# Log-sum-exp over rows on one core: a small Ln moved from ahead of the last exp to behind it

## The chip, the cores and the metric

One core of one Trainium2 chip. The metric is the device time of one execution in microseconds (us), median of several runs; lower is better. Two times are kept apart below: the time of a run (162.5 us) and the span of the profiled execution (161.2 us, the instructions alone).

## The reference

```python
x = np.random.randn(32, 512, 1024).astype(np.float32)       # axis = -1
x_max = np.max(x, axis=axis, keepdims=True)
return (x_max.squeeze(axis) + np.log(np.sum(np.exp(x - x_max), axis=axis))).astype(np.float32)
```

16384 rows of 1024 numbers: 128 rows on each of 128 partitions. The kernel leaves out the maximum and computes log(sum(exp(x))).

## The kernel before

The input comes in 17 chunks of rows through a ring buffer. ScalarE takes the exp. The sums of most rows are made by VectorE, those of the others by ScalarE itself: an exp with an accumulator output, followed by a read of the accumulator. The last four chunks have one row each and go the second way, with their sums in the tile `late`, which lies in PSUM; the ring, the other sums (`sums`) and the result (`res`) lie in SBUF. Both are memories on the chip. Three Ln instructions make the result: 81 rows in the middle of the kernel, 43 rows near its end, the last 4 rows at the end.

```python
CHUNKS = [                       # rows, rows summed by VectorE, parts, by halves
    (4, 4, 1, False), (15, 15, 1, False), ...
    (7, 7, 1, True), (5, 4, 1, True), (4, 3, 1, True), (3, 3, 1, False), (2, 2, 1, True),
    (1, 0, 1, False), (1, 0, 1, False), (1, 0, 1, False), (1, 0, 1, False),
]
LATE = 4
...
    def take_logs(lo, hi, src, dve_wait, act_wait):
        nonlocal acts
        nc.scalar.wait_ge(act_done, act_wait)
        nc.scalar.wait_ge(dve_done, dve_wait)
        nc.scalar.activation(out=res[:, lo:hi], in_=src, func=Ln).then_inc(act_done, 1)
        acts += 1
...
    for i, (r, n_dve, parts, by_halves) in enumerate(CHUNKS):
        if i:
            load(i)
        s, row = place[i]
        ...
        if i == len(CHUNKS) - 1:
            take_logs(logged, late_row, sums[:, logged:late_row], *done_before[-LATE])
        nc.scalar.wait_ge(landed[i], 16)
        ...                                  # exps whose sums VectorE makes
        for j in range(n_dve, r):
            nc.scalar.activation(out=ring[:, s + j], in_=ring[:, s + j], func=Exp,
                                 accum_out=total(row + j)).then_inc(act_done, 1)
            acts += 1
        done_before.append((dves, acts))

    take_logs(late_row, NB, late[:, : NB - late_row], dves, acts)
    nc.sync.wait_ge(act_done, acts)
    nc.sync.dma_start(out=out_v, in_=res).then_inc(stored, 16)
```

The softmax here doesn't subtract the row's maximum and nothing guards it: scores larger than these inputs give would overflow.

## Time and profile before

| | before |
|---|---|
| time, first three runs | 162.53 us median (162.44 to 162.91) |
| span of the profiled execution | 161.2 us |
| DMA of the input | 67.11 MB, mean 417 GB/s over the span |
| ScalarE (ACT) / VectorE (DVE) busy | 115.1 / 121.0 us |

The page's totals and slices, the chain and ScalarE's timeline of the tail stand in the prediction.

### The profile page before, as it was taken

How to read it: one execution, taken by the hardware profiler on the slowest of the kernel's cores; microseconds unless marked ns; L12 is line 12 of the kernel's file. 1: busy time of each engine (PE TensorE's matmuls, PEld its weight loads, DVE VectorE, ACT ScalarE, POOL GpSimd, SP SyncE). 2: the span in 40 equal slices, each digit the busy share in tenths (PEclk: the TensorE clock that was granted, in tenths of full speed). 3: DMA queues.
4: the chain of work that ended last, by engine and by line, in shares of the span. 5: the costliest groups of instructions: out<-in, count | busy, mean ns of one | idle time of the engine just before them, and what ended most of it. 6: DMA issues, size and time to landing. Idle time of an engine off the chain costs nothing.

```text
span 161.2 us, 149 instructions
## 1 busy us (share of the span) xinstructions
DVE 121.0 (75%) x46; ACT 115.1 (71%) x40; POOL 0.2 (0%) x4
## 2 busy tenths in 40 slices
DVE  0028000003999999999999699999999999999892
ACT  3170005996079960999419993999199999999995
POOL 0000000000000000000000000000000000000000
DMA  7999699899899899899889999999899999999990
GB/s 260 504 488 488 290 442 520 374 407 520 374 407 520 374 407 520 374 407 520 374 374 455 455 455 439 423 423 423 385 439 430 434 441 413 418 431 415 409 406 32
DMA packets 2592, 67.18 MB, mean 417 GB/s; under 512 B 288, under 2 KB 416, under 8 KB 928
## 3 DMA queue, kind: packets, MB, share of 16 engines
q1 hardware_dynamic: 2592, 67.18, 97.2%
HBM read 67.11 MB, written 0.07 MB: 417 GB/s over the span
## 4 chain that ended last, share of the span: by engine, by line
DMA 48%; DVE 29%; ACT 20%; issue 0%
DMA ring<-in_x_dram 48%; DVE sums L157 29%; ACT ring L137 17%; ACT ring L164 3%; ACT res L108 0%
## 5 line engine op out<-in xcount | busy, mean ns | idle before, releaser
L157 DVE TENSOR_REDUCE sums<-ring 128x8 f32<-128x8192 f32 (+5 forms) x14 | 111.2, 7994 | 37.1 <-ACT ring L137 37.0
L137 ACT ACTIVATE ring<-ring 128x8192 f32<-128x8192 f32 (+6 forms) x18 | 104.4, 5835 | 43.1 <-DMA ring<-in_x_dram 42.9
L144 DVE CUSTOM_DVE_ANT_0 ring<-ring 128x512 f32<-128x512 f32 x16 | 9.9, 686 | 0.0
L164 ACT ACTIVATE ring<-ring 128x1024 f32<-128x1024 f32 x9 | 9.3, 1042 | 0.0
L122 ACT ACT_TABLE_LOAD x1 | 1.3, 1283 | 1.4 <-PEq L70 1.4
L164 ACT ACTIVATION_READ_ACCUMULATOR ring<-ring 128x1 f32 x9 | 1.6, 174 | 0.0
L144 DVE DVE_READ_ACCUMULATOR2_ANT sums<- 128x1 f32 x16 | 1.3, 83 | 0.0
L108 ACT ACTIVATE res<-sums 128x81 f32<-128x81 f32 (+1 forms) x2 | 0.5, 248 | 0.0
L108 ACT ACTIVATE res<-late 128x4 f32<-128x4 f32 x1 | 0.2, 173 | 0.0
L209 POOL MEMSET const-bfloat16-1.0<- 128x1 bf16 x1 | 0.1, 101 | 0.0
L209 POOL MEMSET const-uint8-127<- 128x1 uint8 x1 | 0.1, 101 | 0.0
L209 POOL MEMSET const-float32-0.0<- 128x1 f32 x1 | 0.1, 98 | 0.2 <-issue 0.2
L209 POOL MEMSET const-float32-1.0<- 128x1 f32 x1 | 0.1, 98 | 0.0
## 6 DMA issues: line engine op xcount, KB each, us to landing
ring<-in_x_dram SPq DMA_DIRECT2D x1, 7680.0 KB, 24.4
ring<-in_x_dram SPq DMA_DIRECT2D x1, 7168.0 KB, 28.6
ring<-in_x_dram SPq DMA_DIRECT2D x1, 6656.0 KB, 35.7
ring<-in_x_dram SPq DMA_DIRECT2D x1, 4608.0 KB, 20.3
ring<-in_x_dram SPq DMA_DIRECT2D x2, 2048.0 KB, 16.0
ring<-in_x_dram SPq DMA_DIRECT2D x1, 3584.0 KB, 28.3
ring<-in_x_dram SPq DMA_DIRECT2D x1, 2560.0 KB, 27.3
ring<-in_x_dram SPq DMA_DIRECT2D x4, 512.0 KB, 27.0
```

The costliest lines, as they stand in the source:

```text
L108: nc.scalar.activation(out=res[:, lo:hi], in_=src, func=Ln).then_inc(act_done, 1)
L122: nc.scalar.preload_act_table_set("natural_log_exp_and_others")
L137: nc.scalar.activation(out=ring[:, s + lo : s + hi], in_=ring[:, s + lo : s + hi], func=Exp).then_inc(act_done, 1)
L144: nc.vector.tensor_tensor_reduce(out=ring[:, s + j, : D // 2], in0=ring[:, s + j, : D // 2], in1=ring[:, s + j, D // 2 :], scale=1.0, scal ...
L157: nc.vector.reduce_sum(out=sums[:, row + lo : row + hi], in_=ring[:, s + lo : s + hi], axis=AX).then_inc(dve_done, 1)
L164: nc.scalar.activation(out=ring[:, s + j], in_=ring[:, s + j], func=Exp, accum_out=total(row + j),).then_inc(act_done, 1)
L209: nc = _bacc.Bacc("TRN2", target_bir_lowering=False, num_devices=1)
```

## The change

Its intent: behind the last exp ScalarE waits for the read of its accumulator before it can take the last Ln. The Ln of 43 rows, whose sums are ready earlier, is to fill that wait, in place of delaying the last exp.

```diff
-        if i == len(CHUNKS) - 1:
-            take_logs(logged, late_row, sums[:, logged:late_row], *done_before[-LATE])
         nc.scalar.wait_ge(landed[i], 16)
...
-    take_logs(late_row, NB, late[:, : NB - late_row], dves, acts)
+    last_sum = acts
+
+    take_logs(logged, late_row, sums[:, logged:late_row], *done_before[-1 - LATE])
+    take_logs(late_row, NB, late[:, : NB - late_row], dves, last_sum)
```

The last Ln still waits for the last accumulator's read (`last_sum`), not for the moved Ln.

## The prediction

> **What bounds the kernel now.** I read the page from the top, then the chain of waits, then ScalarE's own timeline of the last microseconds, and last the raw record of the same trace, which has nanoseconds and the semaphore instructions that the views leave out.
>
> The page's totals and slices:
>
> ```profile
> span 161.2 us, 149 instructions
> ...
> DVE 121.0 (75%) x46; ACT 115.1 (71%) x40; POOL 0.2 (0%) x4
> ...
> DVE  0028000003999999999999699999999999999892
> ACT  3170005996079960999419993999199999999995
> POOL 0000000000000000000000000000000000000000
> DMA  7999699899899899899889999999899999999990
> GB/s 260 504 488 488 290 442 520 374 407 520 374 407 520 374 407 520 374 407 520 374 374 455 455 455 439 423 423 423 385 439 430 434 441 413 418 431 415 409 406 32
> ```
>
> A slice is 161.2 / 40 = 4.03 us. The DMA row is full until the last slice: the kernel streams 67 MB in at about 420 GB/s, and the input load alone fills some 157 of the 161 us. Only in the last slice does DMA fall to 0 and ScalarE (ACT) still works. So the body is a stream from memory, and the change, which touches two small Ln instructions of ScalarE, can only act in the tail after the stream. One of the Lns (128x43) and its place are all that moves; loads, exps and VectorE's sums stay in order, as the comparison of the two programs' instruction lists shows.
>
> The chain of work that ended last, its final pieces (columns: start us, duration us, what):
>
> ```profile
> 146.98 2.76 ACT ring L137
> 149.74 1.04 ACT ring L164 x2
> 150.78 4.46 ACT ring L137 x2
> 155.24 3.02 ACT ring L164 x6
> 158.25 0.01 ACT res L108
> 158.26 0.01 issue
> 158.28 1.11 ACT ring L164 x2
> 159.39 0.02 issue
> 159.42 0.17 ACT res L108
> ```
>
> From 146.98 us the chain is ScalarE without a break: the data for the last chunks had landed and ScalarE works through a backlog. Whatever shortens ScalarE's sequence here shortens the kernel. The piece "ACT res L108" is given 0.01 us only, because the chain hands time to the instructions by their overlapping ends; what the Ln really pushes has to be read from start to start, in ScalarE's timeline of the tail (start, duration):
>
> ```profile
> 156.14 1.04 ACT L164 ACTIVATE ring<-ring 128x1024 f32<-128x1024 f32 x1
> 157.09 0.16 ACT L164 ACTIVATION_READ_ACCUMULATOR ring<-ring 128x1 f32 x1
> 157.14 1.05 ACT L164 ACTIVATE ring<-ring 128x1024 f32<-128x1024 f32 x1
> 158.09 0.17 ACT L164 ACTIVATION_READ_ACCUMULATOR ring<-ring 128x1 f32 x1
> 158.14 0.24 ACT L108 ACTIVATE res<-sums 128x43 f32<-128x43 f32 x1
> 158.28 1.04 ACT L164 ACTIVATE ring<-ring 128x1024 f32<-128x1024 f32 x1
> 159.22 0.16 ACT L164 ACTIVATION_READ_ACCUMULATOR ring<-ring 128x1 f32 x1
> 159.42 0.17 ACT L108 ACTIVATE res<-late 128x4 f32<-128x4 f32 x1
> ```
>
> An exp with its accumulator's read takes 1.00 us from start to start (156.14, 157.14, 158.14). The last exp starts 1.14 us after the one before it, because Ln 128x43 sits between: 0.14 us. After the last exp comes the only gap: the read starts at 159.22, and the last Ln, which needs that read's result, not before 159.42.
>
> **What the Trainium skill says, and whether this trace agrees.** "Perfetto Trace Analysis", section "DVE / Act Engine Instruction (TENSOR_ADD, Activation, etc)": a record runs from the start in the ALUs to the acknowledgement of the write, at which the semaphore is pushed; the next instruction may prefetch before that. The trace agrees: an exp starts some 0.05 us after the start of a read whose record lasts 0.16 us, but the last Ln, which waits for the read's semaphore, starts only after the read's end. In the raw record that end is 159.226 + 0.158 = 159.384 us and the Ln starts at 159.417, 33 ns later.
>
> "ScalarE: Activation LUTs", section "What ACT_TABLE_LOAD costs": an activation takes 186 ns + 0.833 ns per element, and back-to-back ones overlap by about 93 ns. For 1024 elements that is 1039 ns (the page: 1042). For 43 it is 222 ns (the trace: 241); the overlap here is 241 - 142 = 99 ns. The same page's section on table sets has exp and Ln in one set, and the trace has one table load, at the start, with Exp and Ln already interleaved; another order adds none.
>
> "Advanced Engine Details and Errata", section "Engine Queue Depths": ScalarE queues 8 instructions, so waits can be met ahead of time. The trace agrees so far: the separate wait of the last Ln for VectorE passed at 158.249 us, 1.17 us before that Ln started.
>
> "DMA: Bandwidth & Descriptors", section "Anatomy of one DMA": about 2 us fixed for a transfer, mostly the receipt of the write. It tells of another issuing path; here the store is issued at 159.616 and the wait for it ends at 161.178, 1.56 us, and nothing in the change touches it.
>
> **The change, part by part**, from the raw record's nanoseconds.
>
> 1. Removed: Ln 128x43 ahead of the last exp. It started at 158.138 and the exp at 158.280, so it held the exp back by 142 ns. Without it the exp starts one exp period after the exp before: 157.140 + 0.998 (the period from 157.140 to the Ln's start at 158.138) = 158.138 us. Gain of this step: 0.142 us.
>
> 2. Read of the last accumulator: it started 946 ns after its exp (158.280 to 159.226) and took 158 ns. Now 158.138 + 0.946 = 159.084, ending at 159.242.
>
> 3. Added: the same Ln 128x43 behind that read. It does not wait for it: its waits are for sums finished before. As in the kernel before, it starts 51 ns after the read's start (158.087 to 158.138): 159.084 + 0.051 = 159.135. Its 142 ns from start to start free the engine at 159.277.
>
> 4. The last Ln needs both: the read's semaphore, 159.242 + 0.033 = 159.275, and a free engine, 159.277. They meet within 2 ns, so the Ln of 43 rows fills the wait almost exactly: start at about 159.28, against 159.417. Net 0.14 us earlier. (Without the moved Ln the gap from read start to last Ln is 191 ns; an instruction that needs 51 + 142 = 193 ns fits in it.)
>
> 5. Everything behind moves along: last Ln 173 ns, store issue, 1.56 us to the store's landing. The span becomes 161.19 - 0.14 = 161.05 us, and the time 162.53 - 0.14 = 162.39 us.
>
> Beside the path: VectorE's last sum, which Ln 128x43 needs, ends at 157.960 + 0.081 = 158.041. ScalarE's wait for it passed at 158.073 and the Ln started at 158.138, so it held nothing up by more than the few ns by which I cannot tell a decode from a wait. In the changed kernel this sum has one more exp, 1 us, to spare.
>
> **The rivals.**
>
> *The wait is only exchanged: the moved Ln delays the last one.* If the last Ln, queued behind it, cannot have its wait checked until the moved one has ended, it starts at 159.135 + 0.241 + 0.033 = 159.409, and the gain is 8 ns. For it: the queue is in order. Against it: ScalarE's exp started at 158.280 while the Ln before it ended at 158.379, so an end of record doesn't block the next one. The time would be 162.5.
>
> *A wait on VectorE was part of the path.* The wait's pass at 158.073 is only 65 ns ahead of the Ln's start. In an execution in which VectorE ends a little later, the kernel before is held there and the changed one is not; the gain would be 0.14 us plus that lag, perhaps 0.2 in all (an estimate: 0.14 plus an equal 65 ns), time 162.3. Against it: the start at 158.138 follows the read by the same 51 ns as the exps follow theirs.
>
> *The store hides it.* If the store's landing depended on the end of the last loads, ScalarE's end would not matter. Against it: the DMA row is at 0 in the last slice, and the store is issued 26 ns after the last Ln's end at 159.590. I give it little.
>
> *The noise is greater than the effect.* The three runs of before lie between 162.44 and 162.91, 0.47 us apart, over three times the gain. A median of a few runs can then fall on either side of 162.53.
>
> **Range and chances.** The central sum is 162.39, rounded to 162.4. The mechanism gives 162.3 to 162.5; the spread of runs adds about 0.2 downward and 0.3 upward, since the runs of before lean upward (two at 162.44 and 162.53, one at 162.91). That makes 162.1 to 162.75. Two per cent would be 3.25 us. The whole stretch from the start of the removed Ln to the store's issue is 159.616 - 158.138 = 1.48 us, so no gain in it reaches 2%, and a loss would need a new wait of over 3 us, for which nothing is placed. Within 2%: 0.99; half a per cent each for the others.
>
> **What would show it.** In the changed kernel's profile: four exps in line at 1.00 us, the last without a 1.14; Ln 128x43 about 0.05 us after the last read's start; the last Ln some 0.14 us after that, no more than about 0.04 us after the read's end; the busy times of ScalarE and VectorE unchanged at 115.1 and 121.0. Step 1 is wrong if the last exp still starts over 1.00 us after the one before. Steps 3 and 4 are wrong if Ln 128x43 waits for the read's end, or the last Ln for that Ln's end. The total would be wrong if the stream itself moved, by another arrival of the last chunks, or if the store took other than 1.56 us.

## More of the kernel before

One view that the prediction did not ask for is added here, because the argument turns on it: busy time by stretches of one microsecond in the tail of the kernel before (stretch in us, its length, busy us of VectorE, ScalarE and GpSimd with the number of instructions, TensorE's clock, the busy share of the DMA engines, GB/s).

```profile
156.00:157.00 1.00, 1.00 (x2) 1.00 (x3) 0.00 (x0) 1.00 1.02 406
157.00:158.00 1.00, 1.00 (x4) 1.00 (x3) 0.00 (x0) 1.00 0.29 115
158.00:159.00 1.00, 0.04 (x2) 1.00 (x4) 0.00 (x0) 1.00 0.00 0
```

In such a row the DMA share of a stretch says when the input stops moving. It does not say when a load counts as landed: that is when the last of its 16 semaphore increments arrives.

## The result, and the profile after

| | before | after |
|---|---|---|
| time, 6 runs each | 162.49 us median (162.42 to 162.91) | 162.59 us median (162.49 to 162.74) |
| ratio | | 1.0003, 95% interval 0.999 to 1.0016: same |

A ratio is the mean time of one kernel's fast runs over that of the other's of the same rounds, so it is not quite the ratio of the medians quoted.

The page of the changed kernel, the lines that answer to those of before:

```profile
span 161.3 us, 149 instructions
...
DVE 121.0 (75%) x46; ACT 115.0 (71%) x40; POOL 0.2 (0%) x4
```

The busy times are the same, as expected. ScalarE's timeline of the tail (start, duration):

```profile
156.26 1.04 ACT L161 ACTIVATE ring<-ring 128x1024 f32<-128x1024 f32 x1
157.20 0.15 ACT L161 ACTIVATION_READ_ACCUMULATOR ring<-ring 128x1 f32 x1
157.25 1.05 ACT L161 ACTIVATE ring<-ring 128x1024 f32<-128x1024 f32 x1
158.20 0.16 ACT L161 ACTIVATION_READ_ACCUMULATOR ring<-ring 128x1 f32 x1
158.34 1.06 ACT L161 ACTIVATE ring<-ring 128x1024 f32<-128x1024 f32 x1
159.30 0.15 ACT L161 ACTIVATION_READ_ACCUMULATOR ring<-ring 128x1 f32 x1
159.35 0.23 ACT L107 ACTIVATE res<-sums 128x43 f32<-128x43 f32 x1
159.48 0.17 ACT L107 ACTIVATE res<-late 128x4 f32<-128x4 f32 x1
```

The Ln of 43 rows now lies behind the last exp's read and the last Ln follows it at once: that half of the change does what it was meant to. But the last exp does not come 1.00 us after the exp before it. It comes at 158.34, which is 1.08 us after 157.25, although nothing stands between them any more. The gap hides well. The exp before it had its read recorded from 158.20 to 158.36, past the start of the last exp, so ScalarE shows no idle time and the list of waits does not name this one. Only the distance from start to start shows it: 0.05 us from the read to the next exp elsewhere, 0.14 us here.

Some pieces near the end of the chain of waits in the changed kernel (start us, duration us, what) had no counterpart before:

```profile
158.36 0.07 issue
158.43 0.02 ACTq L106
158.45 0.85 issue
```

"issue" is time for which the profile finds no cause; ACTq is ScalarE's sequencer at a separate wait. They are not a new cost: the timeline above has the last exp in the same 0.85 us. The chain was followed back through that separate wait, which now passes after the start of the last exp and not ahead of it. So the chain does not name the cause either. The raw record has the semaphore increments of every load too (read here with times 1 ns below those that the prediction quotes):

```
us from the span's start                    before     after
landing of the last load (its 16th)         158.217    158.312
start of the exp before the last            157.139    157.253
start of the last exp                       158.279    158.335
start of the last Ln                        159.416    159.482
end of the last instruction                 161.194    161.268
```

In the changed kernel the last exp starts 23 ns after the last load's landing. That is the theory to be tested, the **landing theory**: the last load, not ScalarE, set the start of the last exp, and the Ln removed from ahead of it had for the most part been hidden in the wait for that load. The rival, the **engine theory**: something in ScalarE's own queue (the other order, the separate waits) costs the 84 ns (1.082 - 0.998), whatever the load does. A third, that all of it is scatter, is checked by repeats.

### The profile page after: what moved, and what is told of

The parts are those of the page before. It is cut to its first block, busy times and chain, and to the rows that moved or that the text cites. A ratio compares the mean times of both kernels' runs of the same rounds, so it can differ in the third digit from the quotient of the medians.

```text
span 161.3 us, 149 instructions
## 1 busy us (share of the span) xinstructions
DVE 121.0 (75%) x46; ACT 115.0 (71%) x40; POOL 0.2 (0%) x4
## 4 chain that ended last, share of the span: by engine, by line
DMA 48%; DVE 29%; ACT 20%; issue 1%; ACTq 0%
DMA ring<-in_x_dram 48%; DVE sums L154 29%; ACT ring L134 17%; ACT ring L161 3%; ACT res L107 0%; ACTq L106 0%
```

## The experiments

Eight kernels, all correct, on two chips: the first four on one, the others on another. The unchanged kernels were not profiled on the second chip, so there each kernel is compared with its partner, or with the other chip. From the raw record of each one's profile (us):

| kernel | last landing | last exp less exp before | last exp less landing | last Ln less last exp | last Ln less landing |
|---|---|---|---|---|---|
| before | 158.217 | 1.140 | 0.062 | 1.137 | 1.199 |
| after | 158.312 | 1.082 | 0.023 | 1.147 | 1.170 |
| before_again | 158.327 | 1.140 | 0.078 | 1.132 | 1.210 |
| after_again | 158.653 | 1.086 | 0.022 | 1.148 | 1.170 |
| before_scalar_behind | 158.408 | 1.126 | 0.375 | 1.148 | 1.523 |
| after_scalar_behind | 158.175 | 0.997 | 0.246 | 1.149 | 1.395 |
| before_late_load | 158.529 | 1.787 | 0.023 | 1.148 | 1.171 |
| after_late_load | 158.615 | 1.796 | 0.023 | 1.149 | 1.172 |
| before_ln_twice | 157.982 | 1.271 | 0.182 | 1.128 | 1.310 |
| after_ln_twice | 157.861 | 1.098 | 0.022 | 1.270 | 1.292 |

### before_again and after_again: the scatter

No edit. The two kernels once more.

> The kernel before, unchanged, as a measure of the scatter. All theories: ratio 1.000, spread of the runs a few tenths of a microsecond. Last exp 1.14 us after the one before it, last Ln 1.137 us after the last exp. Landing theory: the last load's landing lies some 0.06 us ahead of the last exp, give or take 0.1.

> The changed kernel, unchanged. Landing theory (the last exp is held by the landing of the last load): the last exp starts 20 to 30 ns after that landing and 1.00 to 1.15 us after the exp before, whichever the landing gives. Engine theory (something in ScalarE's own queue, not the load, delays the last exp): 1.08 us again, whatever the landing. Both: last Ln 1.147 us after the last exp; time within 0.15 us of the kernel before.

Measured: before_again 162.66 us median (162.64 to 163.01), ratio 1.0011 (0.9998 to 1.0024); after_again 162.5 us (162.45 to 162.94), ratio 0.9997 (0.9983 to 1.001); the kernel before in the same rounds 162.66 us (162.36 to 162.79). This time the changed kernel has the lower median, so the order of the medians is scatter. The profiled execution of after_again was a long one (162.94 us), and its last load landed at 158.653, 0.34 us later than in the first profile of the same kernel; its last exp came 22 ns after that landing and 1.086 us after the exp before, nearly as in the first profile. Scatter is thus mostly in the arrival of the data, and what follows the landing repeats to within 11 ns: 1.170 and 1.170 us to the last Ln in the changed kernel, 1.199 and 1.210 before. The repeat alone does not decide between the theories, since 1.086 us fits both.

### before_scalar_behind and after_scalar_behind: the load out of the way

Two spare Ln are put ahead of the last four exps, so that ScalarE comes to the last exp later than its data. (In this diff and the next ones the allocation of the spare tile is left out.)

```diff
+        if i == len(CHUNKS) - LATE:
+            for k in range(2):
+                nc.scalar.activation(out=spare[:, k], in_=sums[:, :logged], func=Ln)
         nc.scalar.wait_ge(landed[i], 16)
```

> Two spare Ln of 128x81 put ahead of the last four exps, so that ScalarE runs about 0.32 us later and the last load has landed long before the last exp. Both theories for the order of before: last exp 1.13 to 1.14 us after the one before, last Ln 1.137 us after it; time 0.3 us above the kernel before.

> The same spare Ln in the changed kernel. Landing theory: the load no longer holds the last exp, so it starts 1.00 us after the one before, not 1.08, and the last Ln 1.14 to 1.15 us after it: the full 0.13 to 0.14 us of the prediction appears, against the same spare Ln in the order of before. Engine theory: 1.08 us again, and a gain of 0.05 us only. Times: 0.13 us (landing) or 0.05 us (engine) below before_scalar_behind.

ScalarE's timeline of the tail, before_scalar_behind:

```profile
157.66 1.05 ACT L168 ACTIVATE ring<-ring 128x1024 f32<-128x1024 f32 x1
158.60 0.16 ACT L168 ACTIVATION_READ_ACCUMULATOR ring<-ring 128x1 f32 x1
158.65 0.24 ACT L109 ACTIVATE res<-sums 128x43 f32<-128x43 f32 x1
158.78 1.05 ACT L168 ACTIVATE ring<-ring 128x1024 f32<-128x1024 f32 x1
...
159.93 0.17 ACT L109 ACTIVATE res<-late 128x4 f32<-128x4 f32 x1
```

and after_scalar_behind:

```profile
157.42 1.05 ACT L165 ACTIVATE ring<-ring 128x1024 f32<-128x1024 f32 x1
158.37 0.16 ACT L165 ACTIVATION_READ_ACCUMULATOR ring<-ring 128x1 f32 x1
158.42 1.06 ACT L165 ACTIVATE ring<-ring 128x1024 f32<-128x1024 f32 x1
159.37 0.17 ACT L165 ACTIVATION_READ_ACCUMULATOR ring<-ring 128x1 f32 x1
159.42 0.25 ACT L108 ACTIVATE res<-sums 128x43 f32<-128x43 f32 x1
159.57 0.17 ACT L108 ACTIVATE res<-late 128x4 f32<-128x4 f32 x1
```

With the same order of instructions as the changed kernel, the last exp now follows after 0.997 us: 0.05 us after the read's start, as elsewhere. The engine theory expected 1.08 and falls. From the exp before the last to the last Ln it is 1.126 + 1.148 = 2.274 us in the one and 0.997 + 1.149 = 2.146 us in the other: 0.128 us gained, close to the 0.142 predicted. So the full gain is there as soon as ScalarE, and not the load, is what the end waits for. The times fit, within their scatter: 163.0 us median (162.8 to 163.11), ratio 1.0025 (1.0012 to 1.0037), against 162.81 (162.67 to 162.93), ratio 1.0015 (1.0003 to 1.0028). Between them lie 0.19 us by the medians and 0.10 by the ratios, where the landing theory expected 0.13 and the engine theory 0.05. The two intervals overlap, so the gain is shown by the traces, not by the times.

Two details were expected wrong. In before_scalar_behind the last Ln came 1.148 us after the last exp, not 1.137: the record of the read was 171 ns long, not 158. And the last exp came after 1.126 in place of 1.13 to 1.14 us. The Ln holds the last exp back by 1.126 - 0.997 = 0.129 us when nothing else interferes, so some 0.01 us of the 0.142 read off the kernel before was something else. There the separate wait for VectorE passed at 158.072, only 65 ns ahead of the Ln's start; here it passed at 158.272, 0.38 us ahead of it. That the late pass is the cause is a guess, which no experiment tested alone. The other traces fit it: where the wait passed 62 to 65 ns before a Ln of 43 rows, the next instruction started 142, 143 and 145 ns after that Ln (before, before_again, the first Ln of before_ln_twice); where it passed at least 0.12 us before and neither a load nor the read held the next one, 128 or 129 ns (here, the second Ln of before_ln_twice, both of after_ln_twice).

### before_late_load and after_late_load: the load still later

A spare load is put ahead of the last one, so that the last load lands later. The list `landed` gets one more semaphore for it, so `landed[-1]` is not that of the last load.

```diff
+        if i == len(CHUNKS) - 1:
+            nc.sync.dma_start(out=spare, in_=x_v[:, 0, :512]).then_inc(landed[-1], 16)
         if i:
             load(i)
...
+    nc.sync.wait_ge(landed[-1], 16)
     nc.sync.wait_ge(act_done, acts)
```

> A spare load of 128x512 put ahead of the last load, so that the last load lands about 0.6 us later. Landing theory: the Ln between the last exps is hidden in the wait for the load; the last exp starts 20 to 30 ns after the landing, the last Ln 1.14 us after it; time 0.5 to 0.6 us above the kernel before.

> The same spare load in the changed kernel. Landing theory: the last exp again 20 to 30 ns after the landing, the last Ln 1.14 to 1.15 us after it, so no gain against before_late_load, at most 0.01 us either way. Prediction's step 1 (the removed Ln gives 0.142 us): 0.14 us faster.

ScalarE's timeline, before_late_load (in brackets: idle time before the instruction, and what ended it):

```profile
157.77 0.24 ACT L109 ACTIVATE res<-sums 128x43 f32<-128x43 f32 x1
158.55 1.06 ACT L167 ACTIVATE ring<-ring 128x1024 f32<-128x1024 f32 x1 [0.55 <-DMA ring<-in_x_dram]
```

and after_late_load:

```profile
158.64 1.06 ACT L164 ACTIVATE ring<-ring 128x1024 f32<-128x1024 f32 x1 [0.69 <-DMA ring<-in_x_dram]
```

The wait for the load is now long enough to outlast the records around it, and the profile names it. In the order of before the Ln lies inside the wait: the idle time is 0.55 us in place of 0.69, and the exp starts 23 ns after the landing in both. From landing to last Ln it is 1.171 and 1.172 us. The change gains nothing, as the landing theory had it; step 1 of the prediction would have had 0.14 us. By how much the spare load delayed the last one is not known, for want of an unchanged profile on this chip; that ScalarE now waited for it is what the test needed. Times: 162.94 us (162.82 to 163.56), ratio 1.0035 (1.0018 to 1.0052), and 162.91 us (162.85 to 163.44), ratio 1.0034 (1.0019 to 1.005), over 162.38 us (162.18 to 162.87) of the kernel before in the same rounds.

### before_ln_twice and after_ln_twice: how much room is left

The Ln of 43 rows a second time, directly behind the first, into a spare tile (`take_logs` gets one more argument, the tile to write; a first form that wrote the same tile twice had a race). In the kernel before:

```diff
             take_logs(logged, late_row, sums[:, logged:late_row], *done_before[-LATE])
+            take_logs(logged, late_row, sums[:, logged:late_row], *done_before[-LATE], spare)
```

and in the changed kernel:

```diff
     take_logs(logged, late_row, sums[:, logged:late_row], *done_before[-1 - LATE])
+    take_logs(logged, late_row, sums[:, logged:late_row], *done_before[-1 - LATE], spare)
     take_logs(late_row, NB, late[:, : NB - late_row], dves, last_sum)
```

> The Ln of 43 rows a second time (into a spare tile) directly behind itself, ahead of the last exp. Landing theory: no slack is left for the second, so it costs all of its 0.13 to 0.14 us: last exp 1.27 to 1.28 us after the one before, 0.15 to 0.25 us after the landing; time up 0.13 us.

> The Ln of 43 rows a second time behind the last exp, ahead of the last Ln. If one Ln fills the wait for the accumulator's read exactly (step 4 of the prediction), the second costs all of its 0.13 to 0.14 us: last Ln 1.28 us after the last exp, not 1.15; time up 0.13 us. If there were room left in the wait, less.

In after_ln_twice the two Ln and the last one stand thus (ScalarE's timeline):

```profile
158.85 0.15 ACT L162 ACTIVATION_READ_ACCUMULATOR ring<-ring 128x1 f32 x1
158.90 0.23 ACT L108 ACTIVATE res<-sums 128x43 f32<-128x43 f32 x1
159.03 0.23 ACT L108 ACTIVATE spare<-sums 128x43 f32<-128x43 f32 x1
159.15 0.16 ACT L108 ACTIVATE res<-late 128x4 f32<-128x4 f32 x1
```

The last Ln comes 1.270 us after the last exp, 0.123 us later than with one Ln (1.147 us, on the other chip): the first filled the wait for the read to within about 0.01 us, and the second has no room. That is step 4 of the prediction. In before_ln_twice the second Ln costs 1.271 - 1.140 = 0.131 us and the last exp starts 0.182 us after the landing: the room ahead of the last exp was used up by the first. The times do not resolve this. They were 162.41 us (162.38 to 162.59), ratio 1.0 (0.9984 to 1.0016), where 0.13 us more was expected, a miss, and 162.74 us (162.25 to 162.88), ratio 1.0021 (1.0002 to 1.004), which is more than expected. Both intervals hold the 0.13 us, a ratio of 1.0008. The landings in these two profiles were the earliest of all (157.982 and 157.861), and the second was the fastest run of its kernel: from profile to profile the arrival of the data differs by more than the Ln costs.

## Why the prediction was right or wrong

The measured median, 162.59 us, lies in the range, and "within 2%" came true. Neither speaks for the mechanism: the range, 162.1 to 162.75, also held the 162.53 of no change at all, and 2% is 3.25 us. The centre, 162.4, rested on a gain of 0.14 us that is not there: the ratio is 1.0003. That 162.59 fell into the range is owed to its width; as far as the mechanism goes it is luck. By its steps:

- **What bounds the kernel: wrong in one place.** "The data for the last chunks had landed and ScalarE works through a backlog" holds for the exps from 146.98 us on, but not for the last one. The last load landed at 158.217 us, later than 158.138, when ScalarE could have started the last exp. The claim was read off the chain, which names no load after 146.98 us. The landings in the same raw record would have shown it before the change was made: of the last four rows the first three had their data 0.71, 0.43 and 0.15 us ahead of the start of their exps (155.143, 156.142 and 157.139 us). The loads came 1.23 to 1.28 us apart and the exps 1.00, so ScalarE gained 0.23 to 0.28 us a row on the data and, without the Ln, would have reached the last row 0.08 us ahead of it. The DMA row does not show this, for the last increment of the last load came 0.45 us after the end of its last packet at 157.769.
- **Step 1: the mis-sized term.** It put the removed Ln at 0.142 us. By the prediction's own sign it is wrong: the last exp still starts 1.082 us after the one before. In the traces the last exp starts no earlier than 0.022 us after the landing, so in the kernel before the removal is worth, as an estimate, 0.062 - 0.023 = 0.039 us in the first profile and 0.078 - 0.022 = 0.056 us in the second. The rest of the Ln had been hidden in the wait for the load. With the load out of the way 0.129 us are measured, with the load still later none.
- **Step 2**: the read started 0.946 us after its exp in the prediction; it is 159.297 - 158.335 = 0.962 us in the changed kernel. Where an exp had to wait for its load it is longer by this 0.016 us; with ScalarE behind it is 0.946 again (158.421 to 159.367). Together with step 4 this takes 0.010 us of the gain back.
- **Step 3**: right. The moved Ln started 0.051 us after the read's start.
- **Step 4**: right. Last Ln 32 ns after the read's end, 134 ns after the moved Ln; the doubled Ln shows that there is no more room.
- **Step 5**: right in form. From the last Ln to the end it is 1.778 us before and 1.786 us after. Measured from the landing of the last load to the last Ln, the gain is 1.199 - 1.170 = 0.029 us, in the repeat 1.210 - 1.170 = 0.040 us.
- **The rivals**: "the moved Ln delays the last one" did not happen. "The wait on VectorE" did not set the start of the Ln, which follows the read by 50 or 51 ns whether its wait passed late (before, before_again) or early (before_scalar_behind); some 0.01 us behind that Ln may be due to it. The fourth, that noise is greater than the effect, is what the times show: landings of the last load lie between 158.217 and 158.653 in the four profiles of the two unchanged kernels. The rival that came true, a load that lands only after the removed Ln began, was not on the list. The prediction had "another arrival of the last chunks" only as a change from one kernel to the other, not as a limit in the kernel before.

What the times themselves cannot show is the remaining gain of 0.03 to 0.04 us, 0.02% of the time; intervals here are over 0.1% wide. It rests on two profiles of each kernel.

## What to carry to other kernels

Before counting the removal of an instruction as a gain, look up when the inputs of the instruction behind it arrive: it can start at the later of the two, and where an engine and a stream finish together, as here, both lie within a tenth of a microsecond. Follow the lead of the landings over the instructions through the last few chunks, for a lead that shrinks by a steady amount tells where it is used up. Judge readiness by the last semaphore increment of a load, not by the end of DMA traffic. Judge waits of some tens of nanoseconds from start to start, since the overlapping record of a neighbour can cover them so that no list of idle time shows them.

## What the Trainium skill lacked or had wrong

- "Perfetto Trace Analysis", section "DVE / Act Engine Instruction (TENSOR_ADD, Activation, etc)": it explains that a record runs to the write's acknowledgement, but not that this tail can cover a wait. In the changed kernel the read's record (158.200 to 158.363 us) covers all of the last exp's wait, to 158.335, and the list of waits does not have it.
- No page has the cost of an accumulator's read on ScalarE: with the sum going to PSUM its record was 147 to 172 ns in the ten profiles and the next instruction could start 50 to 54 ns after the read's start; with the sum going to SBUF 185 to 191 ns and 92 to 94 ns.
- "Advanced Engine Details and Errata", section "Engine Queue Depths": it has the depth of 8 alone. "TensorE: Matmul & The Clock Gate" adds that ScalarE's queue is strictly in order, but no page says that a separate wait behind an exp whose load is missing is held as well. In after_scalar_behind the wait for VectorE, behind that exp, passed at 158.205 us, 30 ns after the load's landing, though the sum that it waits for was done at 158.009.
- "DMA: Bandwidth & Descriptors", section "Anatomy of one DMA": its breakdown is for another issuing path than SyncE's, used here, for which no page has the delay from the last packet to the last increment. Here the 16 increments of the last 512 KB load came over 0.79 us (157.426 to 158.217), the last of them 0.448 us after the end of the last input packet; the 64 KB store took 1.54 to 1.55 us from issue to landing.
